# Early splitting of one FFN panel on ScalarE and POOL, and a finer order of wo, in a diffusion backbone

## The chip, the cores and the metric

The kernel runs on one core of a Trainium2 chip. The metric is the device time of one execution in microseconds, given as the median of three runs. TensorE (PE in the rows) does the matmuls, VectorE (DVE) and ScalarE (ACT) the elementwise work, POOL (GpSimd) a few small operations, and SyncE (SP) issues the transfers.

## The reference

Two layers work on 256 latent tokens of width 1024; a context of 256 tokens goes with them up to the attention. All is float32.

```python
def layer_norm(x, g, b):
    mu = mean(x); var = mean((x - mu) ** 2)
    return (x - mu) * rsqrt(var + LN_EPS) * g + b

def half_step_ffn(x, shift, scale, gate, w_in, w_out, g, b):
    h = x * (1 + scale) + shift
    a, u = split(h @ w_in, 2)                  # 1024 x 5632
    y = (silu(a) * u) @ w_out                  # 2816 x 1024
    return layer_norm(ALPHA * x + 0.5 * gate * y, g, b)

for i in range(2):
    m = silu(c) @ ada_w[i] + ada_b[i]          # nine vectors of 1024: shifts, scales, gates
    x = half_step_ffn(x, m[0], m[1], m[2], ...)
    y = neighbourhood_attention(...) if i == 0 else short_conv_mixer(...)   # 16 heads; both end in @ w_out
    x = layer_norm(ALPHA * x + m[5] * y, ...)
    x = half_step_ffn(x, m[6], m[7], m[8], ...)
```

## The kernel before, in words

The 256 tokens are two tiles of 128, tile 0 and tile 1. A product in float32 is made of three matmuls in a shorter format: each operand is split into a high part (a rounded copy) and a low part (what is left), and high x high, high x low and low x high are summed in PSUM (`mmu`, lines 159, 160 and 162). A weight matrix is streamed in units of two K chunks of 128 rows by 512 columns. For each unit `wunit` issues the transfer into a raw buffer (tag wr, four of them), ScalarE copies the high part in two halves (L181: w1h, woh, w2h) and VectorE subtracts it to get the low part (L184: w1l, wol, w2l). The high and low parts have buffers of their own with five, and a few more, copies.

A compile-time scheduler sets the order of all instructions on each engine, by the order of the code and by priorities; each engine then runs its own list in order. TensorE's list is the order of the code. The low part of the activations is made in the same way (`split`, L108 and L109: hTh, hTl, pT, oT, gh, gl).

The program runs an FFN for latents and context, then attention, then the FFN of layer 0 behind it, the first FFN of layer 1, the convolution mixer and the last FFN. The place of the change is the seam between attention and the FFN behind it. The attention loop works through 32 steps (a head and a tile each). For each step scores are made, and two steps later `probs_T` transposes the probabilities (L848) and splits them (pT); one step behind that `values` multiplies them with v (L860, L861, PSUM tile o) and adds two copies of it into osum (L866 on ScalarE, L867 on VectorE); for every second head osum is split into oT, which is the operand of the output matrix wo. wo itself is worked off inside the last steps as filler: `last_filler` makes a generator of its units in the order of `order_late`, (tile, column half, unit), and nine of them are run before the loop ends. The last unit, heads 12 to 15, needs the last oT.

When a bank of wo is complete, `sub_end` calls `residual`: one pass multiplies the bank with the gate (L315), one adds it to x (L319), one gathers the statistics (L321). After both column halves of a tile, `finish_stats` combines the statistics (L328, BN_AGGR) and POOL computes the reciprocal deviation rs (L330, L331); `modulated` normalises x (L339), TensorE transposes it (L347, hT), ScalarE applies the modulation (L353, h) and makes hTh, VectorE makes hTl. Only then the FFN's first panel, w1, can start for this tile. `panels` runs the eleven panels of w1, four units each for either tile; `sil` is the gated product (L403 on ScalarE, L404 on VectorE). After the panels comes w2.

Beside this a background (`stream`, `ada`) computes the modulation vectors of later layers: transfers of 512 KB (ar, three buffers), two accumulating passes each on VectorE (L250 for the first slab, L252 for the others) and a reduction on TensorE (L270). `set_background` gives it a rate in steps per matmul group; `tick` counts them and `drain`, called behind the panels and ahead of w2, runs what is left. On POOL there are few things: the bias of the attention (`bias_pair`, L742), rs, and a memset.

Of the kernel before, what the change touches and what calls it, by code (L numbers as in the profile page):

```python
# [62 lines left out]
E2 = (0, 5, 7)  # L63


@with_exitstack
def backbone_kernel(
# [23 lines left out]
    def nm(s):  # L91
        uid[0] += 1
        return f"{s}_{uid[0]}"
# [54 lines left out]
    def set_background(gen, rate):  # L148
        background[:] = [gen, rate, 0.0]
# [15 lines left out]
    def wunit(srcs, kn, s):  # L165
# [25 lines left out]
    def wpair(w, u, c0, c1, s):  # L191
# [3 lines left out]
        return wunit([(src[:, :, c0:c0 + 256], 0), (src[:, :, c1:c1 + 256], 256)], UK, s)  # L195
# [117 lines left out]
    def residual(ps, xt, gate, wgt, alpha, stats=None):  # L313
        t = sp.tile([P, 512], F32, tag="tmp", bufs=3, name=nm("res"))[:, 0:ps.shape[1]]
        nc.vector.scalar_tensor_tensor(out=t, in0=ps, scalar=wgt, in1=gate, op0=ALU.mult, op1=ALU.mult)  # L315
        if alpha is None:
            nc.vector.tensor_tensor(out=xt, in0=xt, in1=t, op=ALU.add)
        else:
            nc.vector.scalar_tensor_tensor(out=xt, in0=xt, scalar=alpha, in1=t, op0=ALU.mult, op1=ALU.add)  # L319
        if stats is not None:  # L320
            nc.vector.bn_stats(stats, xt)  # L321
# [4 lines left out]
    def finish_stats(st):  # L326
        mv = sm.tile([P, 2], F32, tag="mv", bufs=6, name=nm("mv"))
        nc.vector.bn_aggr(mv, st)  # L328
# [46 lines left out]
    def panels(cols, w, hTs, order, done, s):  # L375

        units, banks = {}, {}
# [55 lines left out]
    def order_late(nu):  # L433
# [3 lines left out]
        o = [(t, n, u) for t, n in banks for u in range(e - 1)]  # L437
        o += [(t, n, u) for u in (e - 1, e) for t, n in banks]
        return o + [(1, 1, u) for u in range(nu)]

    def out_gemm(w, lhs, nk, order, evac, s, wrow0=0):

# [3 lines left out]
        for t, n, u, *c in order:  # L446
            b = (t, n, *c)
            k0, kn = u * UK, min(UK, nk - u * UK)
# [8 lines left out]
            mmu(ps, [(*lhs(k0 + i, t), hi[:, i, cs], lo[:, i, cs]) for i in range(kn)], first, u == ends[b])  # L457
            if u == ends[b]:
# [190 lines left out]
    def sub_end(w, lhs, nk, l, i, gm, wgt, nxt, s, order):  # L649
# [7 lines left out]
        def evac(t, n, bank, *c):  # L657
            if n == 0:
# [4 lines left out]
                     None if part and not c else st[t][:, n + (c[0] // 256 if c else 0)])  # L663
# [12 lines left out]

        return out_gemm(w, lhs, nk, order, evac, s), hTs, (lambda: new_x(l, i))
# [9 lines left out]
    def ffn(hTs, later, l, j, i, gm, nxt):  # L687
# [12 lines left out]
        run(panels([(p * 256, FF + p * 256) for p in range(NP)], ffn_w_in[l, j], hTs, lead_in(NP), done2, "w1"))  # L700
# [139 lines left out]
    PT = {}  # L840

    def probs_T(h, qt, pr):
# [6 lines left out]
        split(pt.rearrange("p (k q) -> p k q", k=4), pth[:, :, qt * P:(qt + 1) * P], ptl[:, :, qt * P:(qt + 1) * P])  # L849
# [3 lines left out]
    def values(h):  # L853

        pth, ptl = PT.pop(h)
        ps = mmb("o")[:, 0:256]
# [11 lines left out]
        if h % 2:  # L868
# [4 lines left out]
            split(osum[0], *(z[:, cs] for z in oT[h // 4]))  # L873
# [15 lines left out]
    def last_filler():  # L889
        with tc.issue_after(bias_dma[-1].ins):  # L890
# [4 lines left out]
            gen, nh, lt = sub_end(na_w_out[0], lhs_T(oT), KC, 0, 1, 5, 1.0, (0, 6), "wo", order_late(KU))  # L895
# [18 lines left out]
    for i in range(len(steps) + LAG + V_LAG):  # L914
# [28 lines left out]
    run(fill)  # L943
    run(fin)
# [7 lines left out]
    set_background(stream([(1, 1, 0), (1, 2, 0)], [(1, 3, 0)]), 0.35)  # L952
    hTs, later = ffn(hTs, later, 0, 1, 2, 8, (1, 0))
# [121 lines left out]
```

## Time and profile before

| what | value |
|---|---|
| median of three runs | 1275.84 us (1275.02, 1275.84, 1280.09) |
| profiled execution | 1277.77 us |
| its span in the trace | 1276.0 us |
| TensorE busy | 1247.6 us, 98% of the span |
| VectorE busy | 955.0 us, 75% |
| ScalarE busy | 591.2 us, 46% |
| POOL busy | 42.1 us, 3% |
| mean granted TensorE clock | 0.997 |

The span runs from the first to the last instruction of the trace; the execution's own time is 1.8 us longer. Busy shares are means over the whole program: a stretch with waits is found in the windows and in the timeline of one engine, where a row gives its start, its length and, in brackets, how long the engine stood idle ahead of it and which instruction released it.

### The profile page before, as it was taken

Reading aid. Unit: us, or ns where it says so; the run is one execution under the profiler, and the core shown is the slowest. Engines: PE = TensorE matmul, PEld = TensorE weight load, DVE = VectorE, ACT = ScalarE, POOL = GpSimd, SP = SyncE. Lnnn points to the kernel's source line nnn. Section 1 sums busy time; section 2 is a strip of 40 time slices with the busy share of each in tenths; the row PEclk is TensorE's granted clock in tenths of the full one; section 3 lists DMA queues with packets and bytes.
Section 4 is the critical chain, followed back from the end, with each engine's and each line's share of the span. In section 5 each row is a group of like instructions: output and inputs, shape, how many; then the busy total and the mean of one; then the engine's idle time right before and its main releaser. Section 6 shows DMA issues by size and latency. Waiting matters only on the chain.

```text
span 1276.0 us, 17190 instructions
## 1 busy us (share of the span) xinstructions
PE 1247.6 (98%) x5890; PEld 1004.9 (79%) x5890; DVE 955.0 (75%) x1683; ACT 591.2 (46%) x1148; POOL 42.1 (3%) x71
## 2 busy tenths in 40 slices
PE   7999999999999999988999999999999999999997
PEld 4787778788778887766887787887787877788886
DVE  4699877485658767788998788867778787865545
ACT  2433132413236456686655435655435644655431
POOL 0000000000001111120000000000000000000000
PEclk9999999999999999999999999999999999999999
DMA  9977668484622744464999888777886764675641
GB/s 295 299 230 244 182 198 296 134 299 147 198 82 74 216 91 91 92 150 129 315 331 313 302 292 281 234 223 228 283 296 221 235 211 133 217 228 186 228 160 54
DMA packets 202712, 268.59 MB, mean 210 GB/s; under 512 B 30026, under 2 KB 149298, under 8 KB 202624
## 3 DMA queue, kind: packets, MB, share of 16 engines
q1 hardware_dynamic: 202624, 267.49, 66.1%
q8 instruction: 46, 0.75, 0.2%
q14 instruction: 42, 0.34, 0.1%
HBM read 265.27 MB, written 2.17 MB: 210 GB/s over the span
## 4 chain that ended last, share of the span: by engine, by line
PE 75%; DVE 10%; DMA 8%; ACT 3%; issue 2%; SPq 1%; POOL 0%; DVEq 0%; ACTq 0%
PE w L159 12%; PE w L162 12%; PE w L160 12%; PE f L553 6%; PE f L554 6%; PE f L555 6%; DMA ar<-in_ada_w_dram 5%; DVE w1l L184 3%; DMA w1r<-in_ffn_w_in_dram 2%; PE wkv L159 2%; PE wkv L160 2%; PE wkv L162 2%; PE wc L159 2%; PE wc L162 2%; PE wc L160 2%
## 5 line engine op out<-in xcount | busy, mean ns | idle before, releaser
L181 ACT ACTIVATE w1h<-w1r 128x512 fp32r<-128x512 f32 x352 | 202.7, 625 | 180.9 <-PE w L162 69.0
L184 DVE TENSOR_TENSOR w1l<-w1r,w1h 128x512 fp32r<-128x512 f32 x352 | 227.3, 685 | 63.5 <-ACT w1h L181 61.3
L159 PE MATMUL w<-w1h,hTh 128*128 128x512 f32 x528 | 209.5, 397 | 1.4 <-ACT hTh L108 1.4
L252 DVE SCALAR_TENSOR_TENSOR acc<-ar,cst,acc 128x512 f32<-128x512 f32 x266 | 187.2, 746 | 31.0 <-DMA ar<-in_ada_w_dram 30.7
L160 PE MATMUL w<-w1l,hTh 128*128 128x512 f32 x528 | 206.0, 390 | 0.0
L159 PE MATMUL w<-w2h,gh 128*128 128x512 f32 (+1 forms) x446 | 173.7, 390 | 0.0
L160 PE MATMUL w<-w2l,gh 128*128 128x512 f32 (+1 forms) x446 | 172.6, 388 | 0.5 <-DVE w2l L184 0.5
L181 ACT ACTIVATE w2h<-w2r 128x512 fp32r<-128x512 f32 x176 | 101.5, 624 | 139.7 <-PE w L162 129.8
L162 PE MATMUL w<-w1h,hTl 128*128 128x512 f32 x528 | 163.2, 390 | 0.9 <-DVE hTl L109 0.9
L184 DVE TENSOR_TENSOR w2l<-w2r,w2h 128x512 fp32r<-128x512 f32 x176 | 114.0, 686 | 43.9 <-ACT w2h L181 42.7
L553 PE MATMUL f<-h0h,w1h 128*128 128x512 f32 x352 | 139.1, 395 | 0.4 <-ACT w1h L181 0.4
L554 PE MATMUL f<-h0h,w1l 128*128 128x512 f32 x352 | 137.5, 391 | 0.0
L555 PE MATMUL f<-h0l,w1h 128*128 128x512 f32 x352 | 137.5, 391 | 0.0
L162 PE MATMUL w<-w2h,gl 128*128 128x512 f32 (+1 forms) x446 | 136.1, 386 | 0.0
L159 PEld LDWEIGHTS w<-w1h,hTh 128*128 128x128 f32 x528 | 99.2, 188 | 24.7 <-ACT hTh L108 2.7
L162 PEld LDWEIGHTS w<-w1h,hTl 128*128 128x128 f32 x528 | 98.9, 188 | 23.0 <-DVE hTl L109 2.1
L160 PEld LDWEIGHTS w<-w1l,hTh 128*128 128x128 f32 x528 | 99.2, 188 | 19.8 <-DVE w1l L184 0.3
L159 PEld LDWEIGHTS w<-w2h,gh 128*128 128x128 f32 x446 | 83.8, 188 | 20.9 <-ACT sil L403 1.7
L160 PEld LDWEIGHTS w<-w2l,gh 128*128 128x128 f32 x446 | 83.8, 188 | 18.2 <-DVE w2l L184 1.9
L162 PEld LDWEIGHTS w<-w2h,gl 128*128 128x128 f32 x446 | 83.4, 188 | 17.1
L553 PEld LDWEIGHTS f<-h0h,w1h 128*128 128x128 f32 x352 | 66.3, 188 | 17.7 <-issue 3.8
L555 PEld LDWEIGHTS f<-h0l,w1h 128*128 128x128 f32 x352 | 66.2, 188 | 14.2 <-DVE h0l L531 0.3
(178 smaller groups left out, 1701.5 us busy)
## 6 DMA issues: line engine op xcount, KB each, us to landing
w1r<-in_ffn_w_in_dram SPq DMA_DIRECT2D x352, 256.0 KB
ar<-in_ada_w_dram SPq DMA_DIRECT2D x128, 512.0 KB
w2r<-in_ffn_w_out_dram SPq DMA_DIRECT2D x88, 512.0 KB
ar<-in_ada_w_dram SPq DMA_DIRECT2D x32, 256.0 KB
wkvr<-in_na_w_qkv_dram SPq DMA_DIRECT2D x32, 256.0 KB
wcr<-in_sc_w_in_dram SPq DMA_DIRECT2D x32, 256.0 KB
wqr<-in_na_w_qkv_dram SPq DMA_DIRECT2D x8, 512.0 KB
bias<-in_na_rpb_dram SPq DMA_DIRECT2D x64, 64.0 KB
```

The costliest lines, as they stand in the source:

```text
L159: nc.tensor.matmul(ps, lh, rh, start=first and i == 0, stop=False)
L160: nc.tensor.matmul(ps, lh, rl, start=False, stop=False)
L162: nc.tensor.matmul(ps, ll, rh, start=False, stop=last and i == n - 1)
L181: nc.scalar.activation(hi[:, a:a + m // W_HI], raw[:, a:a + m // W_HI], AF.Copy)
L184: nc.vector.tensor_tensor(out=lo[:, a:b], in0=raw[:, a:b], in1=hi[:, a:b].bitcast(F32), op=ALU.subtract)
L252: nc.vector.scalar_tensor_tensor(out=a, in0=src, scalar=sc, in1=a, op0=ALU.mult, op1=ALU.add)
L553: nc.tensor.matmul(ps, lh, hT0[k][0], start=(k == 0), stop=False)
L554: nc.tensor.matmul(ps, ll, hT0[k][0], start=False, stop=False)
L555: nc.tensor.matmul(ps, lh, hT0[k][1], start=False, stop=(k == KC - 1))
```

## The change

There are four parts, all around the FFN behind attention.

First, the four units of that FFN's first w1 panel get tiles of their own (16 tiles of the activation pool) instead of the common buffers: `first_unit` calls `wunit` with `own`, a pair of the instructions behind which the splits are queued and of the engine that makes the low parts. The high parts of units 0 and 1 stand on ScalarE behind the last pT, those of units 2 and 3 behind the last oT. The low parts of units 0 to 2 are made on POOL, six instructions of 128x512, queued behind the last bias add; those of unit 3 on VectorE behind the last normalising pass of tile 0. `Parts` lets `mmu` read them as before.

Second, `order_late(nu, True)` takes wo's last unit as two K chunks, each for three banks, so the units become (e, 0) and (e, 1) with three matmuls each. One more of them is run as filler, ahead of the last `probs_T`. The last head's value sum takes its PSUM bank from another tag.

Third, `residual` gets `behind`: where a next sub-layer follows, tile 1's L315 is queued behind tile 0's BN_AGGR, its L319 and L321 behind tile 0's normalising pass. This holds for the w2 seams and for conv's wo as well.

Fourth, this FFN's background has rate 0.4 instead of 0.35, and starts with a negative credit of 24 groups.

```diff
-        o = [(t, n, u) for t, n in banks for u in range(e - 1)]
-        o += [(t, n, u) for u in (e - 1, e) for t, n in banks]
+        o = [(t, n, u) for t, n in banks for u in range(e - 1)] + [(t, n, e - 1) for t, n in banks]
+        if halved:
+            o += [(t, n, (e, i)) for i in range(UK) for t, n in banks]
+        else:
+            o += [(t, n, e) for t, n in banks]
         return o + [(1, 1, u) for u in range(nu)]
...
+    def wunit(srcs, kn, s, own=None):
         raw = wp.tile([P, UN], F32, tag="wr", bufs=WB[0], name=nm(s + "r"))
+        if own:
+            marks, engine = own
+            hs, ls = ([act(F32R, s + c) for _ in range(kn)] for c in "hl")
+            rv = raw[:, :kn * 512].rearrange("p (a b) -> p a b", a=kn)
+            with tc.high_priority(offset=w_early[0]), ExitStack() as st:
+                for src, c in srcs:
+                    sync.dma_start(rv[:, :, c:c + src.shape[2]], src)
+                for i in marks:
+                    st.enter_context(tc.issue_after(i.ins))
+                for i in range(kn):
+                    nc.scalar.activation(hs[i], rv[:, i], AF.Copy)
+                for i in range(kn):
+                    engine.tensor_tensor(out=ls[i], in0=rv[:, i], in1=hs[i].bitcast(F32), op=ALU.subtract)
+            return Parts(hs), Parts(ls)
...
+    def residual(ps, xt, gate, wgt, alpha, stats=None, behind=()):
         t = sp.tile([P, 512], F32, tag="tmp", bufs=3, name=nm("res"))[:, 0:ps.shape[1]]
+        with queued(behind[0:1]):
+            nc.vector.scalar_tensor_tensor(out=t, in0=ps, scalar=wgt, in1=gate, op0=ALU.mult, op1=ALU.mult)
+        with queued(behind[1:2]):
...
+                nc.vector.scalar_tensor_tensor(out=xt, in0=xt, scalar=alpha, in1=t, op0=ALU.mult, op1=ALU.add)
+            if stats is not None:
+                nc.vector.bn_stats(stats, xt)
...
-        ps = mmb("o")[:, 0:256]
+        ps = mmb("o", h == NH - 1)[:, 0:256]
...
-            fill = islice(fin, 9)
+            fill = islice(fin, 10)
         fill_some((n + 1) // 2)
+        if i == len(steps) + LAG - 1:
+            run(fill)
...
     run(fill)
+    run(islice(fin, 1))
+
+    def first_unit(u, behind, engine):
+        return wpair(ffn_w_in[0, 1], u, 0, FF, "w1", (behind, engine))
+
+    own = [first_unit(u, [last_pt[0], bias_dma[1]], nc.gpsimd) for u in range(2)] + [first_unit(2, last_o, nc.gpsimd)]
+    run(islice(fin, 3))
+    own.append(first_unit(3, [last_o[0], norm_ins[1]], nc.vector))
     run(fin)
...
-    def set_background(gen, rate):
-        background[:] = [gen, rate, 0.0]
+    def set_background(gen, rate, hold=0):
+        background[:] = [gen, rate, -rate * hold]
...
-    set_background(stream([(1, 1, 0), (1, 2, 0)], [(1, 3, 0)]), 0.35)
-    hTs, later = ffn(hTs, later, 0, 1, 2, 8, (1, 0))
+    set_background(stream([(1, 1, 0), (1, 2, 0)], [(1, 3, 0)]), 0.4, HOLD)
+    hTs, later = ffn(hTs, later, 0, 1, 2, 8, (1, 0), own)
```

The order of ScalarE behind the last transposed probabilities (pT) before:

```order
L108 ACTIVATE pT_5412<-PT_5434 128x4x128
L866 ACTIVATE osum_5450<-o_5441 64x256
L866 ACTIVATE osum_5450<-o_5453 64x256
L108 ACTIVATE oT_5394<-osum_5450 128x256
L181 ACTIVATE w1h_5590<-w1r_5589 128x512 x2
L181 ACTIVATE w1h_5606<-w1r_5605 128x512 x2
L181 ACTIVATE w1h_5641<-w1r_5640 128x512 x2
L181 ACTIVATE w1h_5621<-w1r_5620 128x512
L353 ACTIVATE h_5545<-hT_5540,gcol_5355 128x128 x4
```

The same place after the change:

```order
L190 ACTIVATE w1h_5490<-w1r_5488 128x512
L916 ACTIVATE osum_5461<-o_5452 64x256
L190 ACTIVATE w1h_5500<-w1r_5499 128x512
L190 ACTIVATE w1h_5501<-w1r_5499 128x512
L916 ACTIVATE osum_5461<-o_5464 64x256
L109 ACTIVATE oT_5394<-osum_5461 128x256
L190 ACTIVATE w1h_5511<-w1r_5510 128x512
L190 ACTIVATE w1h_5512<-w1r_5510 128x512
L190 ACTIVATE w1h_5547<-w1r_5546 128x512
L190 ACTIVATE w1h_5548<-w1r_5546 128x512
L390 ACTIVATE h_5589<-hT_5584,gcol_5355 128x128 x4
```

Two w1h stand ahead of each osum now (the first of them, w1h_5489, one row higher), and the other four between oT and the modulation h.

POOL between the attention's last bias add and tile 1's rs, before:

```order
L742 TENSOR_TENSOR bias_5288<-bias_5288,wmask 128x256
L330 TENSOR_TENSOR rs_5505<-mv_5503,lnc 128x1
L331 TENSOR_TENSOR rs_5505<-rs_5505,lnc 128x1
L258 MEMSET adab_6312 128x512
L330 TENSOR_TENSOR rs_5580<-mv_5578,lnc 128x1
```

And after:

```order
L789 TENSOR_TENSOR bias_5288<-bias_5288,wmask 128x256
L192 TENSOR_TENSOR w1l_5491<-w1r_5488,w1h_5489 128x512
L192 TENSOR_TENSOR w1l_5492<-w1r_5488,w1h_5490 128x512
L192 TENSOR_TENSOR w1l_5502<-w1r_5499,w1h_5500 128x512
L192 TENSOR_TENSOR w1l_5503<-w1r_5499,w1h_5501 128x512
L192 TENSOR_TENSOR w1l_5513<-w1r_5510,w1h_5511 128x512
L192 TENSOR_TENSOR w1l_5514<-w1r_5510,w1h_5512 128x512
L366 TENSOR_TENSOR rs_5541<-mv_5539,lnc 128x1
L367 TENSOR_TENSOR rs_5541<-rs_5541,lnc 128x1
```

The six low parts stand between the last bias add and tile 0's rs.

VectorE at the end of the same FFN's w1 panels, before; acc is the background's accumulator for its last group, sil the gated product (the last two of the panels stand at the end), w2l the low part of w2:

```order
L252 SCALAR_TENSOR_TENSOR acc_6480<-ar_6758,cst,acc_6480 128x512
L184 TENSOR_TENSOR w2l_6880<-w2r_6878,w2h_6879 128x512 x2
L184 TENSOR_TENSOR w2l_6894<-w2r_6892,w2h_6893 128x512 x2
L404 TENSOR_TENSOR sil_6730<-sil_6730,w_1236_6642 128x256
L404 TENSOR_TENSOR sil_6739<-sil_6739,w_1237_6649 128x256
...
L184 TENSOR_TENSOR w2l_6973<-w2r_6971,w2h_6972 128x512 x2
L404 TENSOR_TENSOR sil_6836<-sil_6836,w_1257_6751 128x256
L404 TENSOR_TENSOR sil_6845<-sil_6845,w_1259_6762 128x256
L184 TENSOR_TENSOR w2l_6993<-w2r_6991,w2h_6992 128x512
```

And after:

```order
L278 SCALAR_TENSOR_TENSOR acc_6690<-ar_6843,cst,acc_6690 128x512 x2
L278 SCALAR_TENSOR_TENSOR acc_6690<-ar_6847,cst,acc_6690 128x512 x2
L442 TENSOR_TENSOR sil_6827<-sil_6827,w_1260_6739 128x256
L210 TENSOR_TENSOR w2l_6981<-w2r_6979,w2h_6980 128x512
L278 SCALAR_TENSOR_TENSOR acc_6690<-ar_6851,cst,acc_6690 128x512
L442 TENSOR_TENSOR sil_6840<-sil_6840,w_1261_6746 128x256
L278 SCALAR_TENSOR_TENSOR acc_6690<-ar_6851,cst,acc_6690 128x512
```

The group's last accumulate stood four sil ahead of the end and stands behind the last one now; TensorE's reduction of that group (L270, L296 after) stands between the last w1 matmul and the first w2 matmul in both. The reduction of the first group has moved 104 matmuls back, to 91 matmuls ahead of that.

## Rows read from the trace of the kernel before

**Rows 1.** The page: busy time of each engine, and the chain's shares.

```profile
PE 1247.6 (98%) x5890; PEld 1004.9 (79%) x5890; DVE 955.0 (75%) x1683; ACT 591.2 (46%) x1148; POOL 42.1 (3%) x71
...
PE 75%; DVE 10%; DMA 8%; ACT 3%; issue 2%; SPq 1%; POOL 0%; DVEq 0%; ACTq 0%
```

**Rows 2.** Windows over the seam and later in the same FFN.

```profile
core 0: us, PE busy (x) PEld busy (x) DVE busy (x) ACT busy (x) POOL busy (x), PEclk, DMA share, GB/s
...
580.00:590.00 10.00, 7.21 (x40) 5.52 (x39) 6.27 (x15) 4.07 (x9) 0.00 (x0) 1.00 0.33 106
590.00:600.00 10.00, 9.34 (x43) 6.72 (x41) 9.29 (x18) 7.67 (x17) 1.61 (x3) 1.00 0.25 73
...
680.00:745.00 65.00, 65.00 (x298) 51.61 (x297) 52.02 (x92) 28.94 (x55) 0.00 (x0) 1.00 0.88 309
```

**Rows 3.** Timeline, TensorE: start, us, instruction, count, [idle before <-releaser].

```profile
581.63 0.66 PE L848 MATMUL PT<-ident,pr 128*128 128x128 f32 x4 [0.55 <-DVE pT L109]
...
582.83 0.39 PE L861 MATMUL o<-pT,v 128*128 128x256 f32 x1 [0.42 <-DVE pT L109]
...
584.84 0.39 PE L860 MATMUL o<-pT,v 128*128 128x256 f32 x1 [0.92 <-DVE osum L867]
...
587.43 0.50 PE L159 MATMUL wo<-woh,oT 128*128 128x512 f32 x1 [0.90 <-ACT oT L108]
...
595.73 1.40 PE L347 MATMUL hT<-ident,x 128*128 128x128 f32 x8 [0.25 <-DVE x L339]
...
598.84 0.50 PE L159 MATMUL w<-w1h,hTh 128*128 128x512 f32 x1 [0.32 <-ACT hTh L108]
...
600.66 0.73 PE L162 MATMUL w<-w1h,hTl 128*128 128x512 f32 x2 [0.62 <-DVE hTl L109]
...
610.02 0.50 PE L159 MATMUL w<-w1h,hTh 128*128 128x512 f32 x1 [0.43 <-ACT hTh L108]
```

**Rows 4.** Timeline of POOL, ScalarE and VectorE around the seam.

```profile
554.70 1.20 POOL L742 TENSOR_TENSOR bias<-bias,wmask 128x256 f32<-128x256 f32 x1 [1.60 <-DMA bias<-in_na_rpb_dram]
556.72 0.73 POOL L742 TENSOR_TENSOR bias<-bias,wmask 128x256 f32<-128x256 f32 x1 [0.82 <-DMA bias<-in_na_rpb_dram]
...
593.94 0.52 POOL L330 TENSOR_TENSOR rs<-mv,lnc 128x1 f32<-128x1 f32 x1 [21.55 <-DVE mv L328]
...
586.10 0.38 ACT L866 ACTIVATE osum<-o 64x256 f32<-64x256 f32 x1 [1.76 <-PE o L861]
...
591.43 1.15 ACT L181 ACTIVATE w1h<-w1r 128x512 fp32r<-128x512 f32 x2 [4.05 <-PE wo L162]
...
588.68 0.69 DVE L315 SCALAR_TENSOR_TENSOR res<-wo,gate 128x512 f32<-128x512 f32 x1 [0.85 <-PE wo L162]
...
593.66 0.20 DVE L328 BATCH_NORM_AGGREGATE mv<-st 128x2 f32<-128x12 f32 x1
...
595.13 1.29 DVE L339 TENSOR_SCALAR x<-x,mv,rs 128x512 f32<-128x512 f32 x2 [0.71 <-POOL rs L331]
```

**Rows 5.** Timeline of VectorE, ScalarE and TensorE at the end of w1.

```profile
711.88 0.74 DVE L252 SCALAR_TENSOR_TENSOR acc<-ar,cst,acc 128x512 f32<-128x512 f32 x1
...
729.11 0.42 DVE L404 TENSOR_TENSOR sil<-sil,w 128x256 f32<-128x256 f32 x1 [0.84 <-ACT sil L403]
...
728.70 0.38 ACT L403 ACTIVATE sil<-w 128x256 f32<-128x256 f32 x1 [0.97 <-PE w L162]
...
728.59 1.05 PE L270 MATMUL ada<-acc,ones 128*32 128x512 f32 x4
```

**Rows 6.** Timeline of SyncE and VectorE in the next FFN: one slab.

```profile
911.00 0.46 SPq L239 DMA_DIRECT2D ar<-in_ada_w_dram  x1
...
916.66 0.75 DVE L252 SCALAR_TENSOR_TENSOR acc<-ar,cst,acc 128x512 f32<-128x512 f32 x1 [1.49 <-DMA ar<-in_ada_w_dram]
```

**Rows 7.** Timeline of VectorE at the seam behind this FFN.

```profile
792.17 0.69 DVE L109 TENSOR_TENSOR hTl<-h,hTh 128x512 fp32r<-128x512 f32 x1 [1.56 <-ACT hTh L108]
```

More of the change, by code (lines that the diff above doesn't have):

```diff
@@ L63 @@
 E2 = (0, 5, 7)
+HOLD = 24
 @with_exitstack
@@ L189, in wrows, with wpair @@
         return wunit([(src, 0)], n, s)
-    def wpair(w, u, c0, c1, s):
+    def wpair(w, u, c0, c1, s, own=None):
         if c1 == c0 + 256:
@@ L194, in wpair @@
         src = w[u * UK * P:(u + 1) * UK * P, :].rearrange("(k p) n -> p k n", p=P)
-        return wunit([(src[:, :, c0:c0 + 256], 0), (src[:, :, c1:c1 + 256], 256)], UK, s)
+        return wunit([(src[:, :, c0:c0 + 256], 0), (src[:, :, c1:c1 + 256], 256)], UK, s, own)
     sm.tile([P, PAD], F32, tag="fill", name="fill")
@@ L310, in fold_cols, with queued @@
         return Late(6, rest)
-    def residual(ps, xt, gate, wgt, alpha, stats=None):
-        t = sp.tile([P, 512], F32, tag="tmp", bufs=3, name=nm("res"))[:, 0:ps.shape[1]]
[L315 to L321, printed above, removed]
+    def queued(ins):
+        es = ExitStack()
+        for i in ins:
+            es.enter_context(tc.issue_after(i.ins))
+        return es
+    def residual(ps, xt, gate, wgt, alpha, stats=None, behind=()):
+        t = sp.tile([P, 512], F32, tag="tmp", bufs=3, name=nm("res"))[:, 0:ps.shape[1]]
+        with queued(behind[0:1]):
+            nc.vector.scalar_tensor_tensor(out=t, in0=ps, scalar=wgt, in1=gate, op0=ALU.mult, op1=ALU.mult)
+        with queued(behind[1:2]):
+            if alpha is None:
+                nc.vector.tensor_tensor(out=xt, in0=xt, in1=t, op=ALU.add)
+            else:
+                nc.vector.scalar_tensor_tensor(out=xt, in0=xt, scalar=alpha, in1=t, op0=ALU.mult, op1=ALU.add)
+            if stats is not None:
+                nc.vector.bn_stats(stats, xt)
     def stat_tile(n=2):
@@ L373, in lead_in, with panels @@
         return o + [(t, p, u) for p in range(2, np) for u in r for t in range(2)]
-    def panels(cols, w, hTs, order, done, s):
-        units, banks = {}, {}
+    def panels(cols, w, hTs, order, done, s, own=()):
+        units, banks = {(0, u): x for u, x in enumerate(own)}, {}
         for t, p, u in order:
@@ L447, in out_gemm @@
             b = (t, n, *c)
+            end = u == ends[b]
+            u, *part = u if isinstance(u, tuple) else (u,)
             k0, kn = u * UK, min(UK, nk - u * UK)
@@ L456, in out_gemm @@
             ps = banks[b][:, cs]
-            mmu(ps, [(*lhs(k0 + i, t), hi[:, i, cs], lo[:, i, cs]) for i in range(kn)], first, u == ends[b])
-            if u == ends[b]:
+            mmu(ps, [(*lhs(k0 + i, t), hi[:, i, cs], lo[:, i, cs]) for i in part or range(kn)], first, end)
+            if end:
                 with tc.high_priority(offset=LN_EARLY + (0 if t else T0_EARLY)):
@@ L662, in evac @@
             residual(bank, xt[t][n][:, cs], gate[n][:, cs], wgt, None if c else ALPHA,
-                     None if part and not c else st[t][:, n + (c[0] // 256 if c else 0)])
+                     None if part and not c else st[t][:, n + (c[0] // 256 if c else 0)],
+                     norm_ins if nxt and t else ())
             if n == 1 and (not part or c and c[1] == 512):
@@ L675, in evac @@
                         sync.dma_start(out[0, t * P:(t + 1) * P, h * 512:(h + 1) * 512], xt[t][h])
+        norm_ins.clear()
         return out_gemm(w, lhs, nk, order, evac, s), hTs, (lambda: new_x(l, i))
@@ L685, in lhs_T, with ffn @@
         return f
-    def ffn(hTs, later, l, j, i, gm, nxt):
+    def ffn(hTs, later, l, j, i, gm, nxt, own=()):
         def finish(p, ps):
@@ L698, in done2 @@
                 later()
-        run(panels([(p * 256, FF + p * 256) for p in range(NP)], ffn_w_in[l, j], hTs, lead_in(NP), done2, "w1"))
+        run(panels([(p * 256, FF + p * 256) for p in range(NP)], ffn_w_in[l, j], hTs, lead_in(NP), done2, "w1", own))
         drain()
@@ L840, in backbone_kernel @@
     PT = {}
+    last_pt = []
+    last_o = []
     def probs_T(h, qt, pr):
@@ L848, in probs_T @@
             nc.tensor.transpose(pt[:, k * P:(k + 1) * P], pr[:, k * P:(k + 1) * P], ident)
-        split(pt.rearrange("p (k q) -> p k q", k=4), pth[:, :, qt * P:(qt + 1) * P], ptl[:, :, qt * P:(qt + 1) * P])
+        last_pt[:] = split(pt.rearrange("p (k q) -> p k q", k=4), pth[:, :, qt * P:(qt + 1) * P], ptl[:, :, qt * P:(qt + 1) * P])
     osum = {}
@@ L872, in values @@
             cs = slice((h // 2 % 2) * 256, (h // 2 % 2) * 256 + 256)
-            split(osum[0], *(z[:, cs] for z in oT[h // 4]))
+            last_o[:] = split(osum[0], *(z[:, cs] for z in oT[h // 4]))
     phase.__exit__(None, None, None)
@@ L889, in last_filler @@
     def last_filler():
-        with tc.issue_after(bias_dma[-1].ins):
+        with tc.issue_after(bias_dma[0].ins):
             for t in range(2):
```

21 lines of the change are left out of this document (14 added, 7 removed).

## The prediction

> **What bounds the kernel now.** I read the page first. TensorE works in 1247.6 of 1276.0 us, and three quarters of the chain that ended last are its own matmuls [rows 1]. A change that leaves the number of matmuls alone, as this one does, can therefore win only where TensorE waits, and the question is how much waiting lies where the change works. The windows answer that: 7.21 of 10 us busy from 580 on and 9.34 in the next ten, against 65.00 of 65 later in the same FFN. The granted clock is 1.00 in all of them, so those holes don't cost clock [rows 2]. The window of 65 us holds 298 recorded matmuls, so one takes about 0.22 us. The timeline of TensorE then names eight waits between 581 and 610, together 4.41 us: 0.55 and 0.42 for probabilities, 0.92 for the first copy of a value sum, 0.90 for the last head's oT, 0.25 for tile 0's normalised x, 0.32 and 0.62 for its hTh and hTl, 0.43 for tile 1's hTh [rows 3]. That is the ceiling for the change: 0.35% of the span. Last I looked at what stands beside those waits (ScalarE, VectorE, POOL) and at the end of this FFN's first half, since the change delays the background there.
>
> **The seam, before tile 0's norm.** *Half units of wo.* The 18 matmuls of wo's last unit stood behind the last value sum, and after two of them TensorE waited 0.90 for oT. The change puts three (0.7 us) into the 0.55 wait between the last two transposes. The second wait, 0.42, stays: it ends with the copy of a transposed block that ran earlier. The last head's values no longer wait for the other's bank; they still need their own probabilities, whose copy follows within 0.2 us, so of the 0.92 about 0.8 goes. After them six half-unit matmuls of head pair 12/13 (1.3 us) run while ScalarE and VectorE make the last oT, so of the 0.90 some 0.3 stays. Sum: 0.55 + 0.8 + 0.6 = 1.95 us. *On ScalarE* four of the eight hi splits now stand between the last probability copy and oT. Its waits there are 1.76 ahead of the last osum and 4.05 ahead of the first w1h; two splits take 1.15 [rows 4]. They fit, but they can delay osum by up to 0.3: I take 0.2 off. TensorE reaches the end of wo's six-matmul units for tile 1 about 1.75 us earlier.
>
> **Tile 0's norm is next late.** Its VectorE chain ran from 588.68 to the BN_AGGR at 593.66: eight passes in 4.98 us, 0.62 each [rows 4]. Two of the eight were tile 1's residual, which now waits its turn: 1.25 us, and the chain starts about 0.7 us earlier, since the first bank closes after three matmuls of its last chunk instead of six. BN_AGGR would come near 591.8. Behind it stands POOL's rs, and the change queues six subtractions of 128x512 ahead of that on POOL. No row has one. The nearest is the bias add of half the width: 0.73 alone and 1.20 beside VectorE work [rows 4]. So one lies between 0.73 (if the width were free) and 2.40 (twice the slow one); I take 1.46, twice the quiet one. The first can start when the last transposes (581.63 + 0.66), their copy of about 0.6 and one hi split of 0.58 are over: 583.5. POOL is then free at 583.5 + 6 x 1.46 = 592.3, at 587.9 by the low bound and at 597.9 by the high. Before, rs began at 593.94 [rows 4]. So at my price the norm comes about 1.6 us earlier, half a microsecond later than VectorE would allow. The point at which rs comes no earlier than before is (593.94 - 583.5) / 6 = 1.74 us for one operation.
>
> The slow bias add shows what this rests on: 1.20 against 0.73 in the same loop. The Trainium skill has a rule that speaks against the change: in "SBUF — State Buffer", section "SBUF: two separate sides", a VectorE instruction with two SBUF inputs and a POOL instruction that reads SBUF lock each other out of one port pair for their whole length. The two bias rows agree with it. By that rule every x<-x,res and oT subtraction in these 9 us would add its length to POOL's queue or take POOL's: with three of them POOL is free near 594, the gain of the norm is gone and the sum below would be +2.5 instead of +1.0. The skill's "GPSIMD Engine Reference", section "3.1 Elementwise — side-by-side cycle accounting", puts such an operation at about twice VectorE's time, by an estimate from it 1.3 us instead of my 1.46; POOL would then be free near 591.4 and the sum +0.5. No row here has such an operation.
>
> **From tile 0's norm to tile 1.** L339 started at 595.13 after rs [rows 4]; 1.6 earlier is 593.5, the transposes at 594.1 instead of 595.73. The eight hi splits are gone from ScalarE by then and six lo splits from VectorE, which was busy up to the first hTl. Two splits of unit 3 stay on VectorE in front of hTl, so of the wait of 0.62 I count 0.2 as gained. Tile 1's waits move with it. What is saved at tile 1's first hTl is thus about 1.5 us net, allowing 0.3 for VectorE operations that POOL holds up. Ends: the whole 4.41 if POOL and VectorE don't hinder each other, nothing if rs comes when it did.
>
> **The background's end.** The stream of modulation vectors starts 24 ticks later at rate 0.4. It ends with a reduction on TensorE between the last w1 matmul and the first w2 matmul, in both orders. Before, the last accumulate for it ran at 711.88 and the reduction at 728.59: 16 us to spare [rows 5]. Now the last accumulate stands behind the last sil of the FFN on VectorE, and that sil needs ScalarE's sil, which needs the last w1 matmul. So TensorE must wait where it didn't. From the rows: that sil ends at 729.11 + 0.42 = 729.53 and the accumulate takes 0.74, giving 730.3 instead of 728.59, so 1.7 us. VectorE also has to do all of this group in the 91 matmuls (20 us) between the two reductions: 16 accumulates, 12 halves of w2, 2 gl and 4 sil. With each 0.07 shorter than listed, as the eight passes above follow each other (0.69 listed, 0.62 apart), that is 16 x 0.67 + 14 x 0.62 + 4 x 0.35 = 20.8 us, so I take 2.1. Upper bound: the slabs ar have three buffers, so the last one is loaded only after an accumulate three slabs before. One ar at 911.00 was waited for until 916.66, 5.7 us [rows 6]. If that happens here the wait is about 4. A shorter one than 1.7 needs another order than the one built, so below nothing is excluded. Nothing follows the reduction at once, so w2 starts later by all of it.
>
> **Two smaller places.** At the seam behind this FFN three accumulates now stand ahead of tile 1's first hTl, where one w1l stood less. VectorE waited 1.56 there for hTh [rows 7]; 3 x 0.74 - 0.62 = 1.6 us just fits, unless a slab is late: 0 to 2.0, I take 0.4. At conv's wo seam tile 1's residual waits behind tile 0's norm as well: two passes of 0.62 earlier for tile 0, later for tile 1, with no POOL work beside it: -0.5 to +0.5, I take 0. The rest of the rate change moves VectorE work inside a stretch in which VectorE is busy 52.02 of 65 us [rows 2] and TensorE never waits: nothing, between -0.2 and +0.5.
>
> **Sum.** -1.5 + 2.1 + 0.4 + 0 = +1.0 us: the profiled execution would take 1278.8 instead of 1277.77, its span 1277.0. The median of the three runs before is 1275.84, 1.9 lower than the profiled one, so on that scale the time is 1276.9.
>
> **Rivals.**
> *1. The seam closes and the background hides.* All 4.41 us go, POOL keeps to 0.9 us for one operation, and the wait at the drain is short because sil and accumulate run back to back and later waits swallow part of it (0.5). Time: 1275.8 - 4.4 + 0.5 = 1271.9. For it: ScalarE and POOL are idle in the seam. Against: the built order of the drain.
> *2. POOL becomes the bound of the seam (slower).* Above 1.74 us for one subtraction, rs is later than before and with it everything behind. At 2.40 it comes at 597.9, 4.0 us late; with the drain (2.1) and 0.4 that makes 1275.8 + 6.5 = 1282.3; at 1.9 it is 0.9 + 2.5, 1279.2. For it: the bias add at 1.20, and VectorE's residual lies right in this stretch. Against: the adds without company take 0.73.
> *3. The split doesn't come early.* If raw w1 lands late or ScalarE's fixed order delays oT by as much as the half units gain, the seam gives nothing and only the drain is left: 1275.8 + 2.5 = 1278.3. For it: eight splits are put by hand into a queue that feeds TensorE. Against: ScalarE's first w1h waited for TensorE, not for a DMA [rows 4].
>
> **How the numbers follow.** Forecast 0.56 (1275.0 to 1278.5 by its own ends), rival 1 0.14, rival 2 0.15, rival 3 0.15. The likeliest gives 1276.9. The range takes in rival 3, the smaller gains of rival 1 and the smaller half of rival 2, and the three runs before lie 5 us apart: 1272.5 to 1281.0. A measurement of this kernel can tell about 0.5% from no change, 6.4 us. More than 6.4 us faster would need more than all the waits found: 0.02. More than 6.4 slower happens only at the far end of rival 2 or with a late slab on top: 0.06. Within: 0.92.
>
> **What would show it.** Right: TensorE's waits before 590 shrink from 2.79 to under 1 us, the transposes of tile 0 start near 594, POOL's six rows take 1.3 to 1.6 us each, and the last reduction before w2 is released by VectorE's accumulate, 1.7 to 3 us after the last w1 matmul. Wrong: POOL rows of 2 us or more with rs behind 594; a reduction with no wait; or TensorE waits between 611 and 728 for w1l, which would mean that rate 0.4 overloads VectorE.

## The result and the profile after

| | before | after |
|---|---|---|
| median of 16 runs each | 1277.24 us | 1283.69 us |
| lowest to highest | 1274.70 to 1280.09 | 1278.57 to 1285.96 |
| profiled execution, its span | 1277.77, 1276.0 | 1283.63, 1281.8 |

The ratio is 1.0050 with an interval of 1.0040 to 1.0061: the change makes the kernel 6.4 us slower. The forecast was 1276.9 in a range of 1272.5 to 1281.0, so it missed on the slow side. The forecast was put on the median of three runs, 1275.84; with sixteen runs the kernel before stands at 1277.24. Of the 6.8 us between forecast and measurement 1.4 are thus the base, and 5.4 the change.

The first line of the page of after, against [rows 1]: TensorE's work is the same (1.3 us more), POOL has 7.8 us more, and 4.5 us of the 5.8 us are TensorE waiting.

```profile
PE 1248.9 (97%) x5890; PEld 1005.3 (78%) x5890; DVE 954.2 (74%) x1677; ACT 591.7 (46%) x1148; POOL 49.9 (4%) x77
```

The windows of after, columns as in [rows 2]. The seam is filled up to 590 (9.18 instead of 7.21), and then the hole comes later (7.52 instead of 9.34). What is new stands further down: 2.2 us without TensorE work between 660 and 680, 0.9 in the 65 us that had none, 2.4 at the next seam.

```profile
580.00:590.00 10.00, 9.18 (x49) 6.98 (x48) 7.26 (x14) 7.92 (x16) 6.84 (x6) 1.00 0.58 163
590.00:600.00 10.00, 7.52 (x37) 5.70 (x36) 9.59 (x17) 4.19 (x11) 2.54 (x4) 1.00 0.71 230
660.00:680.00 20.00, 17.80 (x81) 14.06 (x80) 17.43 (x31) 8.78 (x16) 0.00 (x0) 1.00 0.92 308
680.00:745.00 65.00, 64.07 (x290) 50.23 (x289) 46.46 (x82) 28.29 (x53) 0.00 (x0) 1.00 0.77 260
790.00:810.00 20.00, 17.60 (x85) 14.03 (x84) 17.37 (x31) 14.34 (x32) 2.15 (x4) 1.00 0.80 263
```

The kernel before at two of these places: the window from 660, and TensorE's wait at the next seam, which was 0.66 us there:

```profile
660.00:680.00 20.00, 19.80 (x91) 16.16 (x91) 19.01 (x33) 13.35 (x26) 0.00 (x0) 1.00 0.93 319
```

```profile
789.10 1.06 PE L347 MATMUL hT<-ident,x 128*128 128x128 f32 x8 [0.66 <-DVE x L339]
```

The timeline of TensorE in after names the waits (columns as in [rows 3]). Up to 611 they sum to 4.15 us instead of 4.41; those for the last transposes, for osum and for tile 0's hTl are gone, x takes 1.86 instead of 0.25, and tile 1's hTl is new with 0.62:

```profile
582.48 0.39 PE L911 MATMUL o<-pT,v 128*128 128x256 f32 x1 [0.42 <-DVE pT L110]
586.41 0.51 PE L161 MATMUL wo<-woh,oT 128*128 128x512 f32 x1 [0.25 <-ACT oT L109]
595.11 1.08 PE L384 MATMUL hT<-ident,x 128*128 128x128 f32 x8 [1.86 <-DVE x L376]
598.20 0.50 PE L161 MATMUL w<-w1h,hTh 128*128 128x512 f32 x1 [0.62 <-ACT hTh L109]
608.05 0.50 PE L161 MATMUL w<-w1h,hTh 128*128 128x512 f32 x1 [0.38 <-ACT hTh L109]
609.86 0.74 PE L164 MATMUL w<-w1h,hTl 128*128 128x512 f32 x2 [0.62 <-DVE hTl L110]
...
663.41 0.44 PE L450 MATMUL gT<-ident,sil 128*128 128x128 f32 x2 [1.22 <-DVE sil L442]
675.98 0.44 PE L450 MATMUL gT<-ident,sil 128*128 128x128 f32 x2 [0.98 <-DVE sil L442]
730.87 1.95 PE L296 MATMUL ada<-acc,ones 128*32 128x512 f32 x4 [0.93 <-DVE acc L278]
793.25 1.06 PE L384 MATMUL hT<-ident,x 128*128 128x128 f32 x8 [2.19 <-DVE x L376]
961.87 0.51 PE L162 MATMUL w<-w2l,gh 128*128 128x512 f32 x1 [0.90 <-DVE w2l L210]
```

A ledger is made by the start of the same TensorE instruction in both traces, after less before. gT is TensorE's transposes of sil, a fixed point in every panel. Each difference between two lines is what the stretch cost.

| instruction | before | after | after - before | stretch cost |
|---|---|---|---|---|
| value matmul ahead of the seam | 572.29 | 571.93 | -0.36 | |
| first gT behind the seam | 619.72 | 618.62 | -1.10 | -0.74 |
| gT | 721.23 | 722.49 | +1.26 | +2.36 |
| gT behind the reduction, in w2 | 733.80 | 736.96 | +3.16 | +1.90 |
| hT at the next seam | 789.10 | 793.25 | +4.15 | +0.99 |
| gT in the next FFN | 925.30 | 929.74 | +4.44 | +0.29 |
| hT behind that FFN's w2 | 980.18 | 986.50 | +6.32 | +1.88 |
| gT in the last FFN | 1099.57 | 1105.56 | +5.99 | -0.33 |

The seam gains 0.74 us, and the five stretches behind it lose 7.4 us. VectorE's timeline shows how the first of these comes about. It runs its list in order, and in the list an accumulate stands ahead of a sil. When the slab of that accumulate has not landed, everything behind waits for it, the sil of 661 to 663 among them:

```profile
654.37 0.75 DVE L278 SCALAR_TENSOR_TENSOR acc<-ar,cst,acc 128x512 f32<-128x512 f32 x1 [1.19 <-DMA ar<-in_ada_w_dram]
...
658.75 1.42 DVE L278 SCALAR_TENSOR_TENSOR acc<-ar,cst,acc 128x512 f32<-128x512 f32 x2 [1.16 <-DMA ar<-in_ada_w_dram]
660.08 1.29 DVE L210 TENSOR_TENSOR w1l<-w1r,w1h 128x512 fp32r<-128x512 f32 x2
661.29 0.41 DVE L442 TENSOR_TENSOR sil<-sil,w 128x256 f32<-128x256 f32 x1
661.62 1.41 DVE L278 SCALAR_TENSOR_TENSOR acc<-ar,cst,acc 128x512 f32<-128x512 f32 x2
662.94 0.42 DVE L442 TENSOR_TENSOR sil<-sil,w 128x256 f32<-128x256 f32 x1
```

The next stream's first accumulate comes at 740.08 instead of 722.91, since the stream that started late is still being worked off until 731:

```profile
740.08 0.49 DVE L276 TENSOR_SCALAR acc<-ar,cst 128x512 f32<-128x512 f32 x1 [1.16 <-DMA ar<-in_ada_w_dram]
```

In the row of before at that place the releaser is a slab too, 17 us earlier:

```profile
722.91 0.49 DVE L250 TENSOR_SCALAR acc<-ar,cst 128x512 f32<-128x512 f32 x1 [0.89 <-DMA ar<-in_ada_w_dram]
```

### The profile page after: what moved, and what is told of

Its sections match the earlier page's. It is cut to its first block, busy times and chain, and to the rows that moved or that the text cites. A ratio compares the mean times of both kernels' runs of the same rounds, so it can differ in the third digit from the quotient of the medians.

```text
span 1281.8 us, 17197 instructions
## 1 busy us (share of the span) xinstructions
PE 1248.9 (97%) x5890; PEld 1005.3 (78%) x5890; DVE 954.2 (74%) x1677; ACT 591.7 (46%) x1148; POOL 49.9 (4%) x77
## 4 chain that ended last, share of the span: by engine, by line
PE 78%; DVE 8%; DMA 7%; ACT 4%; issue 2%; SPq 1%; POOL 0%; DVEq 0%; ACTq 0%
PE w L161 13%; PE w L164 13%; PE w L162 13%; PE f L598 6%; PE f L599 6%; PE f L600 6%; DMA ar<-in_ada_w_dram 5%; DVE w1l L210 2%; PE wkv L161 2%; PE wkv L162 2%; PE wkv L164 2%; PE wc L161 2%; PE wc L164 2%; PE wc L162 2%; DVE w2l L210 1%
## 5 line engine op out<-in xcount | busy, mean ns | idle before, releaser
L210 DVE TENSOR_TENSOR w1l<-w1r,w1h 128x512 fp32r<-128x512 f32 x344 | 222.0, 687 | 66.1 <-ACT w1h L207 63.4
L207 ACT ACTIVATE w1h<-w1r 128x512 fp32r<-128x512 f32 x344 | 197.3, 624 | 159.4 <-PE w L164 82.8
```

## The experiments

Ratios are to the kernel before, run beside each on the same chip. The late start is the negative credit of 24 groups (`HOLD`), a slab one transfer of the background. **Theory B**: the background's late start and rate make the loss. **Theory P**: POOL's lock on VectorE does. **Theory R**: the early w1 transfers shift the traffic.

**Background as before, the rest as changed (e1).**

```diff
-    set_background(stream([(1, 1, 0), (1, 2, 0)], [(1, 3, 0)]), 0.4, HOLD)
+    set_background(stream([(1, 1, 0), (1, 2, 0)], [(1, 3, 0)]), 0.35)
```

> The changed kernel with the background of the kernel before (rate 0.35, no late start); all else as changed. Theory B (the late, denser background costs the time: 2.1 us at two waits for sil, 1.9 at the reduction, 1.0 at the next seam): these places fall back, only the seam's 1.1 us of gain is left, so 1 us faster than before, ratio 0.998 to 1.000. Theory R (the early w1 transfers shift the DMA traffic, so that slabs land late whatever the background does): the waits for sil near 663 and 676 stay at 1 us each, ratio 1.002 to 1.004. Theory P (POOL's subtractions hold VectorE up and that lag stays): ratio 1.003 or more, with VectorE late at the next panels.

Measured 1.0013 (0.9998 to 1.0028). The waits at the later sil and at the reduction are gone, so R falls, and most of the loss goes with them. B had this run 1 us faster than before, and it is not: by the ledger of its trace the seam gains the same 0.74, but 0.75 go in late sil, 1.5 in a w2l that TensorE waits 1.48 us for at 755.87, and 1.0 in the next FFN's w2.

**The background alone, on the kernel before (e2).**

```diff
-    set_background(stream([(1, 1, 0), (1, 2, 0)], [(1, 3, 0)]), 0.35)
+    set_background(stream([(1, 1, 0), (1, 2, 0)], [(1, 3, 0)]), 0.4, 24)
```

> The kernel before with the changed background alone (rate 0.4, start 24 groups late). Theory B: TensorE waits for VectorE's accumulate ahead of w2 by 1.7 to 2.5 us and for sil twice by about 1 us, so 4 to 7 us slower than before, ratio 1.003 to 1.0055. Theories R and P: nothing but the structural 1.9 us at the reduction, ratio 1.0015.

Measured 1.0099 (1.0067 to 1.0132): the loss is there without any other part of the change, and larger than B put it. In this trace the waits are 2.40 for sil, 0.93 at the reduction and 3.39 for x at the next seam. P falls as the main cause.

**Late start kept, rate of before (e4).** The edit is `0.4, HOLD` to `0.35, HOLD`.

> The changed kernel with the late start kept and the rate of before (0.35). In its order ten accumulates of the last group stand behind the FFN's last two sil. Theory B: the waits for sil near 663 and 676 shrink since fewer slabs are asked for in that stretch, and the wait at the reduction grows from 1.9 to about 7 us (8 more accumulates of 0.67), so 2 to 5 us slower than the changed kernel, ratio to before 1.006 to 1.009. If the rate and not the late start is the cause: faster than the changed kernel.

Measured 1.0126 (1.0099 to 1.0153), more than expected. The timeline of TensorE in this run shows the reduction with the accumulates behind the last sil:

```profile
741.27 2.48 PE L296 MATMUL ada<-acc,ones 128*32 128x512 f32 x4 [9.31 <-DVE acc L278]
```

**Rate 0.4 without the late start (e5).** The edit is `0.4, HOLD` to `0.4`.

> The changed kernel with rate 0.4 and no late start. With the runs at (0.35, none), (0.35, late) and (0.4, late) it completes a square. Theory B1 (the late start is the cost, since it brings the last accumulates behind the last sil): in its order the second group's accumulates lie two panels ahead of w2, so no wait at the reduction, and the time is that of (0.35, none) within 1.5 us, ratio 0.999 to 1.003. Theory B2 (the higher rate is the cost, since slabs are asked for faster than they land): VectorE waits for slabs in front of sil, ratio 1.003 to 1.006.

Measured 0.9987 (0.9975 to 0.9999). The square is closed: with the late start 1.0126 (rate 0.35) and 1.0050 (0.4), without it 1.0013 and 0.9987. The late start is the cause (B1) and the higher rate is not (B2): with the late start it even takes off more than half of the loss.

**Half slabs (e6)**, in the changed kernel: the second half of this FFN's modulation vectors is left out, the first is computed twice.

```diff
-                sync.dma_start(w, ada_w[l, k * P:(k + 1) * P, m * D:(m + 1) * D])
+                wide = 512 if half_slab[0] else D
+                sync.dma_start(w[:, :wide], ada_w[l, k * P:(k + 1) * P, m * D:m * D + wide])
```

> The changed kernel, but the background of this one FFN transfers only the first 512 of 1024 columns of each slab and accumulates them twice, so half of the modulation vectors of the next layer is left out; instructions and order stay. If TensorE's waits for sil (663, 676) and part of the next seam come from slabs that land late: they go, and only the wait at the reduction (about 1.9, set by the order) is left, so 2 to 4 us faster than the changed kernel, ratio to before 1.001 to 1.0035. If they come from VectorE being full (rate 0.4), they stay: ratio 1.0045 to 1.006.

Measured 1.0043 (1.0029 to 1.0056): the time lies between the two, and the trace speaks for the slabs at the place asked for. The waits for sil at 663 and 676 are gone altogether. What they gave (3.1 us by the ledger, from the first gT to 721) was in part lost again at the reduction (1.4 us): the last slab was issued behind a transfer of w2 and landed late all the same, in front of the last sil. The time shows less than this trace, which is of the fastest of ten runs (1278.34; their median is 1281.35), so that the slabs cost the waits for sil is shown at that place and not as a share of the time. VectorE and TensorE in this run:

```profile
726.15 0.75 DVE L282 SCALAR_TENSOR_TENSOR acc<-ar,cst,acc 128x512 f32<-128x512 f32 x1 [1.43 <-DMA ar<-in_ada_w_dram]
726.82 0.41 DVE L446 TENSOR_TENSOR sil<-sil,w 128x256 f32<-128x256 f32 x1
...
727.05 1.95 PE L300 MATMUL ada<-acc,ones 128*32 128x512 f32 x4 [2.32 <-DVE acc L282]
```

**Late starts of 12 and 18 groups (e11, e14)**: `HOLD = 12` and `HOLD = 18` in the changed kernel.

> The changed kernel with half the late start (12 groups). In its order the last accumulate stands two sil ahead of the end, so TensorE needs no wait at the reduction. Theory: the loss of 24 groups has two sources, the order at the reduction with what follows it (2 to 3 us) and slabs that land behind their place in VectorE's list (2 us). Then only the second is left, ratio 1.000 to 1.003. If the delay as such counts (in proportion to the groups): about half of 0.63%, 1.002 to 1.0035. If the order at the reduction is all: 0.9985 to 0.9995.

> The changed kernel with a late start of 18 groups at rate 0.4, between 12 (ratio 0.9993) and 24 (1.005). In its order the last accumulate stands just ahead of the last two sil. If the end is the cause, with a threshold where the accumulate passes the last sil: as with 12 groups, 0.999 to 1.001. If the delay counts in proportion: 1.002 to 1.0035.

Measured 0.9993 (0.9978 to 1.0009) with 12 and 1.0058 (1.0040 to 1.0075) with 18. Between 0, 12, 18 and 24 groups (0.9987, 0.9993, 1.0058, 1.0050) there is a step, not a proportion; and it is not where I put it, since with 18 groups the reduction has no wait. In that run one accumulate of the next stream has moved between the residual passes of tile 0 at the next seam, its slab lands late, and TensorE waits 5.79 us for the normalised x. VectorE and TensorE there:

```profile
785.61 0.68 DVE L350 SCALAR_TENSOR_TENSOR res<-w,gate 128x512 f32<-128x512 f32 x1
788.40 0.75 DVE L278 SCALAR_TENSOR_TENSOR acc<-ar,cst,acc 128x512 f32<-128x512 f32 x1 [2.11 <-DMA ar<-in_ada_w_dram]
789.07 0.68 DVE L355 SCALAR_TENSOR_TENSOR x<-x,res 128x512 f32<-128x512 f32 x1
...
793.63 1.73 PE L384 MATMUL hT<-ident,x 128*128 128x128 f32 x7 [5.79 <-DVE x L376]
```

Of the sixteen traces three have an accumulate between these two passes: the changed kernel, e2 and e14.

**Late start of 24 with rate 0.5 (e13).** The edit is `0.4, HOLD` to `0.5, HOLD`.

> The changed kernel with the same late start (24 groups) and rate 0.5. In its order the last accumulate stands a panel ahead of the end, so there is no wait at the reduction and the next stream starts earlier; but slabs are asked for a quarter faster in the stretch from 640 to 700. If the end (reduction 1.9 us, the next stream's late start 1.0 to 3) is the cause: ratio to before 0.998 to 1.001. If slabs that land behind their place are: the waits for sil and w1l grow beyond 2.1 us, ratio 1.003 to 1.007.

Measured 1.0047 (1.0027 to 1.0067). The reduction has no wait and the loss stays, so the end of the FFN is not all of it. The ratio is the one expected of late slabs, but the growth of the waits beyond 2.1 us did not come: the trace has 0.29 and 1.22 for sil, 1.55 at the next seam and, in two parts, 1.00 for w2l behind that. From the seam to the last FFN it is only 2.1 us slower than the trace of the kernel before, so a good part of the loss in time (some 6 us) is not placed.

**The seam's parts.** In e3 the background is that of before and the low parts of units 0 to 2 are made on VectorE; e9 is the same at rate 0.4 without late start; e7 is e3 with unit 2 behind the norm.

```diff
-    own = [first_unit(u, [last_pt[0], bias_dma[1]], nc.gpsimd) for u in range(2)] + [first_unit(2, last_o, nc.gpsimd)]
+    own = [first_unit(u, [last_pt[0], last_pt[1]], nc.vector) for u in range(2)] + [first_unit(2, last_o, nc.vector)]
```

> The changed kernel with the background of before, and with the low parts of the own units 0 to 2 on VectorE instead of POOL. Read against the run with that background alone. Theory P: the two x<-x,res passes of tile 0 take 1.3 us again instead of 2.76, and though VectorE has six passes more (3.7 us) it does most of them in its idle time ahead of oT and of the first bank, so tile 0's transposes start 0.5 to 1.5 us earlier and the time is 0.5 to 1.5 us shorter. Rival: the six passes themselves stand in front of tile 0's norm and cost what POOL's lock cost: within 0.5 us of it, or up to 1.5 us longer.

> The run with the low parts on VectorE, but unit 2's two low parts behind tile 0's norm like unit 3's, so that only four passes stand ahead of it, in VectorE's idle time. If the low parts in front of the norm set the start of tile 0's transposes: they start 0.6 to 1.2 us earlier, and hTl of tile 0 moves at most 0.6 later, so 0.3 to 1 us faster than that run, ratio to before 0.998 to 0.9985. Rival: hTl becomes the wait instead and nothing is gained: 0.999.

> The changed kernel without the late start (rate 0.4), and with the low parts of units 0 to 2 on VectorE instead of POOL. Theory: the late start was the loss and POOL's lock the second cost (0.4 us of the seam in the pair at rate 0.35: 0.7 gained with POOL, 1.1 without). Then 0.3 to 0.6 us faster than the run at rate 0.4 without late start, ratio to before 0.997 to 0.9985. Rival: which slabs meet which sil after the seam decides more than the seam does (the pair at rate 0.35 differed by 2.4 us for 0.4 us of seam): ratio 1.000 to 1.002.

Measured 0.9989 (0.9974 to 1.0003) for e3, 1.0001 (0.9989 to 1.0013) for e7, 0.9988 (0.9975 to 1.0000) for e9. VectorE in after and then in e3, tile 0's two x<-x,res:

```profile
589.13 2.76 DVE L355 SCALAR_TENSOR_TENSOR x<-x,res 128x512 f32<-128x512 f32 x2
```

```profile
589.48 1.28 DVE L355 SCALAR_TENSOR_TENSOR x<-x,res 128x512 f32<-128x512 f32 x2
```

POOL's subtractions cost 1.48 us on tile 0's path. In the time the two pairs do not agree: at rate 0.4 nothing shows (0.9988 for e9, 0.9987 for e5), at rate 0.35 the run without them is faster (0.9989 for e3, 1.0013 for e1; medians 1275.56 and 1278.89). By the ledger only 0.4 us of that lies in the seam; the waits for sil and w2l that e1 has behind it are missing in e3. Whether the subtractions bring those about is not shown. In e7 x came early (a wait of 0.23) and ScalarE's hTh became the wait (1.96); its rival had said so of VectorE's hTl.

Two parts alone: e8 has the half units on the kernel before, e12 the early split and rate 0.4, and e10 rate 0.4 on the kernel before with nothing else.

> The kernel before with the half units of wo, the tenth filler unit and the other bank alone: no early split, no waiting residual, background as before. TensorE's three waits there (0.55, 0.92, 0.90) shrink by 1.9 us as in the changed kernel. If tile 0's norm on VectorE decides what comes of it: the transposes of tile 0 start only 0.7 us earlier than before (the first bank's lead), and the time falls by 0.3 to 0.9 us, ratio 0.9993 to 0.9998. If the early split is needed for any gain: 1.000. If wo's order alone is the gain: 0.9985.

> The kernel before with the early split of the first panel alone (POOL for units 0 to 2) and rate 0.4: no half units of wo, no waiting residual. If the three parts of the seam only work together: tile 0's norm stays where it was or comes later behind POOL's lock, gain 0 or a loss up to 1 us, ratio 0.9995 to 1.001. If the early split carries the seam's gain alone: 0.9985 to 0.999.

> The kernel before with rate 0.4 and nothing else. If the run at rate 0.4 without late start owes its 0.13% to the seam (0.7 us) and no more: this one stands at 0.9993 to 1.0003. If it owes it to the background's being done earlier: 0.9985 to 0.999, and the seam is worth nothing in the time.

Measured 1.0008 (0.9996 to 1.0020) for e8, 1.0021 (1.0008 to 1.0033) for e12 and 1.0013 (1.0002 to 1.0025) for e10. None gains alone. In e8 the time won by wo goes into waits for w1l (0.60, 1.12), the low parts that are still made late. In e12 the splits on ScalarE stand ahead of oT with no half units to cover them. TensorE then waits for both parts of oT, the high and the low one. The timeline of TensorE in e12:

```profile
588.10 0.50 PE L161 MATMUL wo<-woh,oT 128*128 128x512 f32 x1 [1.67 <-ACT oT L109]
590.29 0.50 PE L164 MATMUL wo<-woh,oT 128*128 128x512 f32 x1 [1.23 <-DVE oT L110]
```

Against e10, which shares its background, e5 is 0.26% faster (0.9987 to 1.0013): the seam's parts together are worth some 3 us there. The traces place 0.7 of it in the seam and about 1 in waits for w1l and sil (0.53 and 0.88 in e10, 0.35 in e5); the rest they do not place. e5 and e9 are the best versions: 0.6% faster than the change as made (about 8 us). Against the kernel before e5 is 0.13% faster, and its interval (0.9975 to 0.9999) just leaves out no change.

## Why the prediction was wrong, point by point

**Half units of wo: right.** Of 0.55 + 0.92 + 0.90 us, 0.25 is left; 2.1 us against the 1.95 of the sum.

**Tile 0's norm: mis-sized, by the mechanism the prediction named.** POOL's six subtractions took 8.17 us, 1.36 each in the mean against 1.46, and were done at 591.3, before BN_AGGR. Of the six the last took 1.73, beside two VectorE passes that took 1.06 and 1.77:

```profile
583.16 8.17 POOL L192 TENSOR_TENSOR w1l<-w1r,w1h 128x512 fp32r<-128x512 f32 x6 [10.86 <-DMA w1r<-in_ffn_w_in_dram]
589.60 1.73 POOL L192 TENSOR_TENSOR w1l<-w1r,w1h 128x512 fp32r<-128x512 f32 x1
593.40 0.19 POOL L366 TENSOR_TENSOR rs<-mv,lnc 128x1 f32<-128x1 f32 x1 [2.07 <-DVE mv L364]
...
589.13 1.06 DVE L355 SCALAR_TENSOR_TENSOR x<-x,res 128x512 f32<-128x512 f32 x1
590.11 1.77 DVE L355 SCALAR_TENSOR_TENSOR x<-x,res 128x512 f32<-128x512 f32 x1
```

POOL waited for VectorE by 2.07 us and not the other way round. I put the cost of their meeting on POOL's queue and allowed 0.3 us for VectorE; the greater part fell on VectorE's passes, 2.76 for two instead of 1.28, so BN_AGGR came at 593.11 and not at 591.8. Rival 2 is thus wrong in its place and right in its cause. The rule of the Trainium skill ("SBUF — State Buffer", section "SBUF: two separate sides") says that the one that comes second stands still. The rows agree in both directions: the pass of 590.11 ends 0.55 us behind POOL's last subtraction, and that one, begun within the pass of 589.13, took 1.73 where the median of the six is 1.29. The transposes came at 595.11 instead of 594.1, and the seam gave 0.74 instead of 1.5 us.

**The reduction: right.** 1.90 us against 2.1, with the chain as told: sil at 730.63, accumulate at 730.96. TensorE's row gives it as a wait of 0.93 and a reduction of 1.95 instead of 1.05, whose second half waits for this accumulate.

```profile
730.63 0.42 DVE L442 TENSOR_TENSOR sil<-sil,w 128x256 f32<-128x256 f32 x1
730.96 0.75 DVE L278 SCALAR_TENSOR_TENSOR acc<-ar,cst,acc 128x512 f32<-128x512 f32 x1
```

**"Nothing" for the rest of the rate change: this step failed, by 2.4 us.** I took VectorE's mean (52.02 of 65 us busy) as cover, over a window that begins at 680; the two large waits lie ahead of it, at 663 and 676. Nor does the mean say much of an engine that runs its list in order: an accumulate whose slab is not there stops it while it is not full. In the window from 660 VectorE was busy 17.43 of 20 us and TensorE lost 2.2; in the kernel before it was busy 19.01 and TensorE lost 0.2. I put this term down to the rate, and the square puts it on the late start: from the first gT to the one behind the reduction the changed kernel loses 4.26 us, e5 with the same rate and no late start 0.41. I had the price of a late slab in [rows 6] (5.7 us from issue to use) and used it for upper ends alone, at the reduction and at the next seam. It applies wherever an accumulate stands ahead of a pass that TensorE needs soon.

**The next seam: 0.99 us against 0.4, and at another place.** I looked at the accumulates ahead of tile 1's hTl; what cost stands among tile 0's residual passes, an accumulate (0.67 us) and one w1l more than before (0.60). It was in the built order and I did not look there.

```profile
788.03 0.75 DVE L278 SCALAR_TENSOR_TENSOR acc<-ar,cst,acc 128x512 f32<-128x512 f32 x1
788.70 0.69 DVE L355 SCALAR_TENSOR_TENSOR x<-x,res 128x512 f32<-128x512 f32 x1
789.30 0.68 DVE L210 TENSOR_TENSOR w1l<-w1r,w1h 128x512 fp32r<-128x512 f32 x1
```

**The next FFN's w2: 1.88 us, not in the sum at all.** The prediction ended the late start's effect with its own FFN. The next stream shares the three buffers and starts 17 us later. Runs without a late start lost between -0.3 and 1.0 us in the same stretch, but e2, with the same late start on the kernel before, gained 0.8 there. How much of it belongs to the late start is not shown.

**Conv's seam: -0.33, inside its ends.** The rivals: 1 and 3 did not happen (oT came early, the reduction waited). "TensorE waits between 611 and 728" was named as what would prove the forecast wrong, for w1l and a full VectorE; it came for sil and a late slab.

The range was too narrow because the rest of the rate change had a spread of only -0.2 to +0.5 us: runs of the changed kernel that differ only in the background's timing lie between 0.9987 and 1.0126.

What stays open: why 18 and 24 groups cost the same while their waits lie in different places. Each background has its own set of accumulates that meet late slabs, and the runs give no rule for which. Open too is why TensorE waits for sil near 663 with a late start of 24 groups and not with 12 or 18.

## What to carry to other kernels

Background work in an in-order list can cost what its latest transfer costs, at every place where foreground work stands behind it: look in the built order for each background instruction that stands ahead of a pass on the critical path, and ask when its data lands, rather than how busy the engine is. Work that was started later to keep a seam clear came out further down, at the end of its stage and at the next seam; change its start alone and time it before it goes in with anything else. Parts that each remove one wait were worth nothing singly and a little together (0.13%), and that only at one of the two rates.

## What the runs showed of the hardware

Two passes of VectorE of 128x512 with two inputs that met POOL's subtractions took 2.76 us instead of 1.28. A subtraction on POOL took 1.29 us in the median and 1.73 where a VectorE pass came first; an estimate from the Trainium skill ("GPSIMD Engine Reference", section "3.1 Elementwise — side-by-side cycle accounting", twice VectorE's time) was 1.3 us. All instructions of POOL's line in after (least, median and longest in ns):

```profile
L192 POOL TENSOR_TENSOR w1l<-w1r,w1h x6: 1272/1294/1732, 583.2 to 589.6; 128x512 fp32r<-128x512 f32 x6
```

The granted clock falls to one half (1.2 of 2.4 GHz) for some microseconds in the attention, after TensorE has waited 0.41 and 1.55 us for pT around 551. Where it begins and ends differs from run to run, though TensorE's code is the same up to there. Two windows over the same stretch, of before and of e1 (PEclk is the third number from the end):

```profile
553.00:557.00 4.00, 3.67 (x16) 2.38 (x14) 4.00 (x10) 2.17 (x5) 1.58 (x3) 0.76 0.54 74
```

```profile
553.00:557.00 4.00, 3.88 (x12) 2.55 (x11) 4.00 (x9) 1.41 (x3) 1.46 (x2) 0.50 0.44 72
```

So a seam behind it must be measured from an instruction after that place, as the ledger does; and single runs of the kernel before differ by 5 us.
